# Keys and values in one 512-column product, values in float32, and four late query tiles, in a two-layer encoder

## The chip, the cores and the metric

The kernel runs as one program on one core of a Trainium2 chip. The core has a matrix engine (PE; its weight loads are shown apart as PEld), a vector engine (DVE), a scalar engine (ACT), a general engine (POOL) and a queue that issues the transfers (SP). Each engine works through its own list of instructions in the order in which they were written, and stops at one whose inputs are not there. The metric is the device time of one execution in microseconds (us).

## The reference

The reference is an encoder of two layers on 1024 tokens of width 1024. Layer 0 mixes the tokens with grouped-query attention (16 query heads, 4 key and value heads of 64 columns); layer 1 mixes them with pooled windows. Both layers then attend to 256 memory tokens and end in a gated network with a short convolution. The change touches the attention of layer 0 alone:

```python
qkv = h @ w_qkv
q, k, v = ...            # 16, 4 and 4 heads of 64 columns
q, k = rmsnorm(q, q_gain), rmsnorm(k, k_gain)
q = apply_axial_rope(q, cos, sin) * (HEAD_DIM ** -0.5)
k = apply_axial_rope(k, cos, sin)
p = softmax(q k^T); o = p v; return o @ w_o
```

## The kernel before

**Precision.** A float32 product is made of three products of a "high" and a "low" part: `mm3` (L757 to L759) issues high*high, high*low and low*high. The high part is a copy on ACT (L670, or L688 with a scale), the low part a subtraction on DVE (L673, or L686 with a scale; L950 for the weights).

**Projection.** `attention` first projects the 8 row tiles of 128 tokens. The normalised tokens are not formed; the transposed input is scaled by a column gain and split (`plan_columns`: ACT L688, DVE L686, in chunks of 128, 128, 256 and 512 tokens), and the factor of each row (`first`, from `plan_rows`: a square on ACT L929, two small steps on POOL L931 and L932) is applied to the results. `QKV` lists the products: ("K", t) and ("V", t) are the 256 key and value columns of row tile t, (g, t) a fourth (256 columns, 4 heads) of the queries, ("S", n) a product of queries and keys for the largest scores. Each product is 8 blocks of 128 rows by 3 matrix instructions of 256 columns into a bank pB. Values are split in high and low (L688, L686).

**The head.** A tile of keys or queries then goes through `plan_head`: a square (ACT L1007), a sum over each head (DVE L1011), two small POOL steps (L730, L732), the scaling of the bank by both factors (DVE L1019), the rotation (DVE L1026 twice, L1030) and its sum (POOL L1034). Then PE turns the tile (L1058 for keys, L1089 for queries), and ACT and DVE split it (L670, L673). `LAG` says how many products later the turn is placed. From key tile 2 on the difference of two key tiles (POOL L1052) is turned too. The head takes its tables from `plan_tables` (POOL L899, L906).

**The loop.** The attention itself runs over 16 groups (a half of the rows, a pair of heads), with 8 tiles of keys in each: `plan_scores` (L1221 into pT, the exponential on ACT L1228), `plan_values` (L1263 into pO, in plain float32), `plan_peaks` (L795 into pS, 3 buffers, and the largest score on DVE L801, a group ahead; in the first four steps three of them a step, later two). The values it needs in float32 are formed at its start by `plan_v32`, high plus low, on POOL (L1203). Then come 2000 us of work that the diff does not touch.

**Who sets the order.** `Plan.run` lays out the projection, and then, apart, the loop. It takes PE's work in the written order; an instruction of another engine gets a due time from the PE work that needs it, and one that no PE work of the same plan needs has none and is laid out at the very end. All instructions of the projection therefore stand ahead of all of the loop on each engine. The loop's banks pS, pT and pO lie where the projection's pA and pB lay, and wait for the last reader of what lay there.

## Time and profile before

| what | us |
|---|---|
| median of 3 runs (2408.22 to 2410.0) | 2409.18 |
| the profiled execution | 2408.76 |
| its span on the core | 2407.0 |
| PE busy | 2386.5 |
| DVE busy | 1888.0 |
| ACT busy | 1181.1 |
| POOL busy | 423.4 |
| projection, first product to last | 5.87 to 166.4 |
| loop, first product | 167.51 |

The execution is a little longer than the span of its instructions. A row of the timeline has the start, the time, the engine, the line, the operation, the tiles out<-in and their shape, and in brackets the idle time ahead of it with what ended that. Instructions of PE overlap: the distance between two starts is what one of them costs. The same holds, less strongly, on the other engines.

### The profile page before, as it was taken

Reading aid. Unit: us, or ns where it says so; the run is one execution under the profiler, and the core shown is the slowest. Engines: PE = TensorE matmul, PEld = TensorE weight load, DVE = VectorE, ACT = ScalarE, POOL = GpSimd, SP = SyncE. Lnnn points to the kernel's source line nnn. Section 1 sums busy time; section 2 is a strip of 40 time slices with the busy share of each in tenths; the row PEclk is TensorE's granted clock in tenths of the full one; section 3 lists DMA queues with packets and bytes.
Section 4 is the critical chain, followed back from the end, with each engine's and each line's share of the span. In section 5 each row is a group of like instructions: output and inputs, shape, how many; then the busy total and the mean of one; then the engine's idle time right before and its main releaser. Section 6 shows DMA issues by size and latency. Waiting matters only on the chain.

```text
span 2407.0 us, 33944 instructions
## 1 busy us (share of the span) xinstructions
PE 2386.5 (99%) x12468; PEld 1934.9 (80%) x12468; DVE 1888.0 (78%) x2689; ACT 1181.1 (49%) x1892; POOL 423.4 (18%) x462
## 2 busy tenths in 40 slices
PE   9999999999999999999999999999999999999998
PEld 9984444688998888888888888898888888888887
DVE  6789999549873798888888768987389888888875
ACT  6335556425562555455454426555255555545442
POOL 6757777410010000000000003011000000000001
PEclk9999999999999999999999999999999999999999
DMA  7000001425951234333387533695124332338752
GB/s 255 19 2 11 19 18 42 152 81 194 318 199 44 90 98 128 109 89 109 99 290 248 180 106 123 219 330 201 58 79 120 99 110 88 117 122 274 257 188 101
DMA packets 323010, 324.06 MB, mean 135 GB/s; under 512 B 32564, under 2 KB 253084, under 8 KB 322844
## 3 DMA queue, kind: packets, MB, share of 16 engines
q1 hardware_dynamic: 322844, 321.90, 41.4%
q8 instruction: 98, 1.61, 0.3%
q14 instruction: 68, 0.56, 0.1%
HBM read 234.35 MB, written 82.64 MB: 132 GB/s over the span
## 4 chain that ended last, share of the span: by engine, by line
PE 92%; DVE 3%; issue 3%; DMA 1%; POOL 1%; ACT 1%; SPq 0%; POOLq 0%; DVEq 0%; ACTq 0%
PE pB L757 23%; PE pB L759 23%; PE pB L758 23%; PE pO L1263 4%; PE pT L1221 3%; PE pA L759 3%; PE pA L757 3%; PE pA L758 3%; PE pS L795 2%; PE pB L326 1%; DVE R L673 1%; PE pS L1299 1%; PE pA L2275 1%; DVE nm L801 0%; POOL scr L1275 0%
## 5 line engine op out<-in xcount | busy, mean ns | idle before, releaser
L757 PE MATMUL pB<-R,R 128*128 128x512 f32 (+1 forms) x2764 | 1024.6, 371 | 2.5 <-ACT R L670 0.8
L759 PE MATMUL pB<-R,R 128*128 128x512 f32 (+1 forms) x2760 | 1017.3, 369 | 1.3 <-DVE R L673 1.2
L758 PE MATMUL pB<-R,R 128*128 128x512 f32 (+1 forms) x2764 | 1018.3, 368 | 0.2 <-DVE R L673 0.2
L757 PEld LDWEIGHTS pB<-R,R 128*128 128x128 f32 x2764 | 521.6, 189 | 93.6 <-ACT R L670 2.0
L759 PEld LDWEIGHTS pB<-R,R 128*128 128x128 f32 x2760 | 520.7, 189 | 89.5 <-DVE R L673 3.0
L758 PEld LDWEIGHTS pB<-R,R 128*128 128x128 f32 x2764 | 521.7, 189 | 86.0 <-DVE R L673 1.2
L670 ACT ACTIVATE R<-scr 128x512 fp32r<-128x512 f32 (+3 forms) x372 | 268.6, 750 | 228.4 <-DMA scr<-Gs 61.1
L730 POOL TENSOR_SCALAR ms<-ss 128x1 f32<-128x1 f32 (+1 forms) x92 | 27.1, 294 | 1648.0 <-ACT R L738 1279.0
L673 DVE TENSOR_TENSOR R<-X,R 128x512 fp32r<-128x512 f32 x374 | 252.4, 686 | 67.5 <-ACT R L670 66.9
L673 DVE TENSOR_TENSOR R<-scr,R 128x512 fp32r<-128x512 f32 (+2 forms) x332 | 283.8, 884 | 20.8 <-ACT R L670 20.7
L670 ACT ACTIVATE R<-X 128x512 fp32r<-128x512 f32 x374 | 231.7, 630 | 132.2 <-PE pB L758 64.0
L440 ACT COPY scr<-pB 128x512 f32<-128x512 f32 x156 | 91.3, 585 | 181.6 <-PE pB L759 174.4
L801 DVE TENSOR_REDUCE nm<-pS 128x1 f32<-128x512 f32 x240 | 152.8, 683 | 18.1 <-PE pS L795 16.7
L1966 DVE TENSOR_TENSOR X<-pB,X 128x512 f32<-128x512 f32 (+1 forms) x145 | 99.4, 687 | 84.9 <-PE pB L759 83.9
L1228 ACT ACTIVATE X<-pT 128x1024 f32<-128x1024 f32 x128 | 125.2, 1023 | 76.2 <-PE pT L1221 72.8
L757 PE MATMUL pA<-R,R 128*128 128x512 f32 (+1 forms) x420 | 150.6, 359 | 0.0
L759 PE MATMUL pA<-R,R 128*128 128x512 f32 (+1 forms) x420 | 150.3, 358 | 0.0
L758 PE MATMUL pA<-R,R 128*128 128x512 f32 (+1 forms) x420 | 149.9, 357 | 0.0
L1263 PE MATMUL pO<-X,X 128*64 128x512 f32 x512 | 123.8, 605 | 0.0
L442 DVE TENSOR_TENSOR scr<-pB,scr 128x512 f32<-128x512 f32 x156 | 106.8, 685 | 12.0 <-PE pB L759 11.9
L1221 PE MATMUL pT<-R,R 64*128 64x512 f32 x768 | 104.8, 393 | 1.0 <-ACT X L1228 1.0
L1811 DVE SCALAR_TENSOR_TENSOR scr<-scr,conv 128x1023 f32<-128x1023 f32 x66 | 84.6, 1282 | 20.8 <-ACT scr L1806 19.0
(179 smaller groups left out, 2872.0 us busy)
## 6 DMA issues: line engine op xcount, KB each, us to landing
X<-in_ffn_w_up SPq DMA_DIRECT2D x82, 512.0 KB
Gs<-X SPq DMA_DIRECT2D x105, 256.0 KB
scr<-in_ffn_w_down SPq DMA_DIRECT2D x45, 512.0 KB
scr<-Gs SPq DMA_DIRECT2D x35, 512.0 KB
scr<-in_xattn_w_kv SPq DMA_DIRECT2D x32, 512.0 KB
scr<-Gs SPq DMA_DIRECT2D x42, 384.0 KB
Wt<-scr SPq DMA_DIRECT2D x44, 256.0 KB
Gs<-scr SPq DMA_DIRECT2D x42, 256.0 KB
```

The source lines that it names most:

```text
L440: self.nc.scalar.copy(out, p)
L442: self.nc.vector.tensor_tensor(out=out, in0=p, in1=out, op=OP.add)
L670: self.nc.scalar.activation(hi, src, AF.Copy)
L673: self.nc.vector.tensor_tensor(out=lo, in0=src, in1=hi.bitcast(F32), op=OP.subtract)
L757: mm(out, ah, bh, start=start, stop=False)
L758: mm(out, ah, bl, start=False, stop=False)
L759: mm(out, al, bh, start=False, stop=stop)
L801: nc.vector.tensor_reduce(NM[G][:, 2 * n + x.start:2 * n + x.stop], S, axis=AX.X, op=OP.max, negate=True)
L1221: nc.tensor.matmul(T[G, kt % 2][:, x * 512:(x + 1) * 512], left, right, start=first and (i, j) == (0, 0), stop=shifted or (not first and i ...
L1228: nc.scalar.activation(E[G, kt], T[G, kt % 2], AF.Exp)
L1263: nc.tensor.matmul(O[G][x * HD:(x + 1) * HD], V32[kt // 4][:, kt % 4, m // 4 * 2 + x], E[G, kt][:, x * 512:(x + 1) * 512], start=kt == 0, ...
L1966: nc.vector.tensor_tensor(out=x, in0=banks[b][:, c], in1=x, op=OP.add)
```

## The change

Keys and values of a row tile become one product of 512 columns, so that pB holds both; all 8 of them come first, then the queries. The weights of both come in 8 blocks, each split on ACT and DVE (none of it on POOL any more). The last chunk of tokens, of 512, becomes two of 256. Values are scaled by ACT straight into float32 tiles; their low part and the sum on POOL are gone. The heads of the last four query tiles, (3, 4) to (3, 7), write to one scratch tile, and are turned and split in steps 1 to 4 of the loop, in the place of a bank pS. The three values of `IDLE` that fill PE with transposes at the start change from 8, 15, 4 and 8 to 8, 28 and 4. In the changed file most lines of the attention are lower or higher by some 2 to 18.

```diff
--- before.py
+++ after.py
-QKV = (("K", 0), ("K", 1), ("V", 0), ("V", 1), ("K", 2), ("V", 2), ("K", 3), ("V", 3),
-       ("K", 4), (0, 0), (0, 1), ("K", 5), (0, 2), (0, 3), ("K", 6), (0, 4), (0, 5), ("K", 7), (0, 6), (0, 7),
-       *(it for n in range(24) for it in ([(1 + n // 8, n % 8), ("S", n // 4)] if n % 4 == 1 else [(1 + n // 8, n % 8)])),
-       ("S", 6), ("V", 4), ("S", 7), ("V", 5), ("V", 6), ("V", 7))
-LAG = 4
+QS = [(g, t) for g in range(2) for t in range(NT)] + [(2 + n // 4 % 2, n % 4 + n // 8 * 4) for n in range(2 * NT)]
+QKV = (*(("K", t) for t in range(NT)), *QS[:9], *(it for n, q in enumerate(QS[9:]) for it in ([q, ("S", n // 2)] if n % 2 == 1 and n < 16 else [q])))
+LAG, LATE = 4, 4
 QN = 4
-POOLED = (2, 3)
+POOLED = ()
-IDLE = {("K", 0, 0): 8, **{("K", 0, g): 5 for g in (1, 2, 3)}, ("K", 1, 0): 4, ("K", 2, 0): 8}
-CHUNKS = ((0, P), (P, P), (2 * P, 2 * P), (4 * P, 4 * P))
+IDLE = {("K", 0, 0): 8, **{("K", 0, g): 4 for g in range(1, 8)}, ("K", 1, 0): 4}
+CHUNKS = ((0, P), (P, P), *((n * P, 2 * P) for n in (2, 4, 6)))
...
-        V = [R.get(), None]
+        X = {t: xv.tile([P, D], F32, name=f"XV{t}") for t in (5, 7)}
+        V32 = [X[t].rearrange("p (k h c) -> p k h c", k=4, h=NKV) for t in (5, 7)]
+        late = [(1, NKV - 1, t) for t in range(NT - LATE, NT)]
...
-            sets = [[qk.tile([P, 2048], F32R, name=f"T{i}") for i in range(2)], [R.get(), R.get()], [R.get(), R.get()]]
+            sets = [[qk.tile([P, 2048], F32R, name="T"), R.get()], [R.get(), R.get()], [R.get() for _ in range(4)]]
...
+            def plan_kv(g):
+                raw = ("wraw", "K", g)
+
+                def high(k):
+                    self.high(kv(0)[k // 4][:, k % 4], at[raw][:, k % 2])
+
+                def low(engine, k):
+                    engine.tensor_tensor(out=kv(1)[k // 4][:, k % 4], in0=at[raw][:, k % 2], in1=kv(0)[k // 4][:, k % 4].bitcast(F32),
+                                         op=OP.subtract)
...
+                    if ks[0] == 0:
+                        at[b] = self.psB() if wide else self.psB()[:, :256]
+                        if wide:
+                            at["v", t] = at[b][:, 256:]
+                    for k in ks:
+                        for _ in range(IDLE.get((*it, k), 0) if k == ks[0] else 0):
+                            nc.tensor.transpose(idle[:, :P], self.ident, self.ident)
+                        self.mm3(at[b], *self.blk(hT[t // 4], k, slice(t % 4 * P, (t % 4 + 1) * P)), *weights(k), k == 0, k == NK - 1)
...
+                cut = [(k,) for k in range(NK)] if it == ("K", 0) else [(k, k + 1) for k in range(0, NK, 2)] if it == ("K", 1) else [range(NK)]
...
             def plan_v(t, b):
-                def part(j):
...
-                    self.hi_lo_half(j, v[:, :, :HD], v[:, :, HD:], src(), first[:, t:t + 1])
-                plan.add("copy", 360, partial(part, 0), [b] + own, [("V", t)], uses=[b], room=None if t < 4 else ("V1", 2))
-                plan.add("add", 340, partial(part, 1), [b, ("V", t)] + own, [("V", t)], uses=[b])
+                def scaled():
+                    nc.scalar.activation(V32[t // 4][:, t % 4], at.pop(("v", t)).rearrange("p (h c) -> p h c", h=NKV), AF.Copy, scale=first[:, t:t + 1])
+                plan.add("copy", 360, scaled, [b, ("first", t)], [("V", t)], uses=[b])
...
                 def scaled():
-                    at[qn] = buf("qn", QN) if kind == "Q" else buf("kr", 4)
+                    if it in late:
+                        at["late"] = at["late"] if "late" in at else self.scr()
+                        i = late.index(it)
+                        at[qn] = late[i] = at["late"][:, 256 * i:256 * i + 256]
+                    else:
+                        at[qn] = buf("qn", QN) if kind == "Q" else buf("kr", 4)
...
                 qn, bank = plan_head(it, "Q", t, b), ("qturned", it)
+                if it in late:
+                    return None
...
+            def plan_late(i):
+                b, t = ("late", i), NT - LATE + i
+
+                def turn():
+                    T[b] = self.ps.tile([P, 512], F32, name="pS", bufs=3)
+                    for h in range(2):
+                        nc.tensor.transpose(T[b][:, h * P:(h + 1) * P], late[i][:, h * P:(h + 1) * P], self.ident)
...
+                    self.low(h, l, p) if lo else self.high(h, p)
+                plan.add("turn", 2, turn, [b], [(b, 0)], [("A", b)], ["late"])
...
-            def plan_v32(s):
...
-                    nc.gpsimd.tensor_tensor(out=V32[s], in0=v4[..., :HD], in1=v4[..., HD:], op=OP.add)
...
-                plan.add("product", 9.2, emit, [*es, ("V32", d // 2)], ["O"],
+                plan.add("product", 9.2, emit, es, ["O"],
...
                     if n:
                         plan_values(*steps[n - 1])
+                    if 1 <= n <= LATE:
+                        plan_late(n - 1)
...
-    arrays["attn_w_qkv"] = np.ascontiguousarray(w.transpose(3, 0, 2, 1, 4)).reshape(-1, P, D)
+    kv = w[:, :, :, NKV:].reshape(4, 2, P, 2 * NKV * HD).transpose(0, 2, 1, 3).reshape(-1, P, D)
+    arrays["attn_w_qkv"] = np.concatenate([w[:, :, :, :NKV].transpose(3, 0, 2, 1, 4).reshape(-1, P, D), kv])
```

What it does to the order is seen at three places. The first is DVE at the end of the projection and the start of the loop. Before, from the head of the last query tile on (qn; R9 holds values, R10 turned queries):

```order
L673 TENSOR_TENSOR R10_77<-pB_2347,R10_77 128x2x128
L686 SCALAR_TENSOR_TENSOR R9_76<-pB_2356,first_109,R9_76 128x4x64
L673 TENSOR_TENSOR R10_77<-pB_2396,R10_77 128x2x128
L686 SCALAR_TENSOR_TENSOR R9_76<-pB_2399,first_109,R9_76 128x4x64
L673 TENSOR_TENSOR R10_77<-pB_2444,R10_77 128x2x128
L1193 MEMSET ones_2507 128x64
L686 SCALAR_TENSOR_TENSOR R9_76<-pB_2447,first_109,R9_76 128x4x64
L673 TENSOR_TENSOR R10_77<-pB_2472,R10_77 128x2x128
L801 TENSOR_REDUCE nm_2523<-pS_2511 128x1
L801 TENSOR_REDUCE nm_2523<-pS_2512 128x1
```

After it (L1033, L1040 and L1044 are now the lines of the head, scr_2170 the scratch tile of the late query tiles):

```order
L1020 TENSOR_REDUCE ss4_2246<-sq_2244 128x4
L671 TENSOR_TENSOR R11_78<-pB_2225,R11_78 128x2x128
L1033 SCALAR_TENSOR_TENSOR scr_2170<-pB_2127,first_113,rs_2253 128x256
L1040 TENSOR_TENSOR rb_2256<-scr_2170,tab_111 128x8x16 x2
L1044 TENSOR_TENSOR scr_2170<-scr_2170,tab_111 128x256
L1033 SCALAR_TENSOR_TENSOR scr_2170<-pB_2172,first_113,rs_2263 128x256
L1040 TENSOR_TENSOR rb_2266<-scr_2170,tab_111 128x8x16 x2
L1044 TENSOR_TENSOR scr_2170<-scr_2170,tab_111 128x256
L1033 SCALAR_TENSOR_TENSOR scr_2170<-pB_2200,first_113,rs_2273 128x256
L1040 TENSOR_TENSOR rb_2276<-scr_2170,tab_111 128x8x16 x2
L1044 TENSOR_TENSOR scr_2170<-scr_2170,tab_111 128x256
L802 TENSOR_REDUCE nm_2314<-pS_2303 128x1
```

Three heads of late query tiles stand between the projection's last turned tile and the loop's first largest score, each behind the POOL steps (rs) of its own; before, value parts stood there.

The second is PE at the same place, with what each instruction waits for. Before:

```order
L759 MATMUL pB_2447<-T0_105,R15_82 128x256
L1089 MATMUL pB_2472<-ident_87,qn_2390 128x128 [waits DVE_49,PE_49,Pool_49]
L1089 MATMUL pB_2472<-ident_87,qn_2390 128x128
L795 MATMUL pS_2511<-R0_67,R16_83 128x512 [waits DVE_49]
L795 MATMUL pS_2512<-R0_67,R16_83 128x512
L1221 MATMUL pT_2516<-R16_83,R0_67 128x512 [waits DVE_49]
```

After:

```order
L757 MATMUL pB_2200<-R4_71,R17_84 128x256
L1105 MATMUL pB_2225<-ident_87,qn_2119 128x128 [waits DVE_49,Activation_49,Pool_49]
L1105 MATMUL pB_2225<-ident_87,qn_2119 128x128
L796 MATMUL pS_2303<-R0_67,R18_85 128x512 [waits DVE_49,Activation_49]
L796 MATMUL pS_2304<-R0_67,R18_85 128x512 [waits PE_49]
L1239 MATMUL pT_2307<-R18_85,R0_67 128x512 x4
```

The first product of the loop now waits for ACT too. Counted in the program, the instruction of DVE that it waits for is the scaling of the last late tile (L1033 out of pB_2200, the third L1033 in the DVE rows above), since pS_2303 lies in a bank of that tile; before, it was the low part of the last value tile (L686 out of pB_2447).

The third is DVE early in the projection, at the heads of key tiles 0 and 1 (kr) and the next chunk of tokens (R with gcol). Before:

```order
L1011 TENSOR_REDUCE ss4_431<-sq_380 128x4
L1030 TENSOR_TENSOR kr_390<-kr_390,scr_300 128x256
L686 SCALAR_TENSOR_TENSOR R3_70<-pB_287,first_109,R3_70 128x4x64
L686 SCALAR_TENSOR_TENSOR R3_70<-pB_334,first_109,R3_70 128x4x64
L1019 SCALAR_TENSOR_TENSOR kr_443<-pB_245,first_109,rs_436 128x256
L1026 TENSOR_TENSOR rb_449<-kr_443,scr_300 128x8x16 x2
L1030 TENSOR_TENSOR kr_443<-kr_443,scr_300 128x256
L1011 TENSOR_REDUCE ss4_484<-sq_445 128x4
L686 SCALAR_TENSOR_TENSOR R13_80<-scr_425,gcol_108,R12_79 128x512 x2
L686 SCALAR_TENSOR_TENSOR R13_80<-scr_438,gcol_108,R12_79 128x512
```

After:

```order
L1033 SCALAR_TENSOR_TENSOR kr_397<-pB_160,first_113,rs_383 128x256
L1033 SCALAR_TENSOR_TENSOR kr_429<-pB_268,first_113,rs_395 128x256
L684 SCALAR_TENSOR_TENSOR R15_82<-scr_374,gcol_112,R14_81 128x256
L1040 TENSOR_TENSOR rb_438<-kr_397,scr_370 128x8x16 x2
L1040 TENSOR_TENSOR rb_442<-kr_429,scr_370 128x8x16 x2
L1044 TENSOR_TENSOR kr_397<-kr_397,scr_370 128x256
L1044 TENSOR_TENSOR kr_429<-kr_429,scr_370 128x256
L1020 TENSOR_REDUCE ss4_452<-sq_433 128x4
L684 SCALAR_TENSOR_TENSOR R15_82<-scr_374,gcol_112,R14_81 128x256 x3
L684 SCALAR_TENSOR_TENSOR R17_84<-scr_385,gcol_112,R16_83 128x256 x4
L1033 SCALAR_TENSOR_TENSOR kr_490<-pB_342,first_113,rs_470 128x256
```

The chunk for row tiles 4 and 5 (R15, R17), eight instructions, now stands behind the heads of both key tiles, and ahead of it all key and value products of the first four row tiles; before, two value tiles stood between the heads.

169 lines of the change are left out of this document (76 added, 93 removed).

## Prediction, made before the run

> **What bounds the kernel now.** The page first, for the bound of the whole: its span, and the chain that ended last.
>
> ```profile
> span 2407.0 us, 33944 instructions
> PE 92%; DVE 3%; issue 3%; DMA 1%; POOL 1%; ACT 1%; SPq 0%; POOLq 0%; DVEq 0%; ACTq 0%
> ```
>
> PE carries 92% of the chain. So a change counts by the PE work that it takes away and by the time in which PE waits. The profiled execution took 2408.76 us, 0.4 below the median of 2409.18; the sum is made against it. 0.2% (4.8 us) is about what a measurement of this kernel can tell from no change.
>
> Next the timeline of PE at the two ends of the projection, since the diff changes nothing behind the loop's second group.
>
> ```profile
> 5.87 0.36 PE L757 MATMUL pB<-T,R 128*128 128x256 f32 x1
> ...
> 6.98 0.71 PE L972 MATMUL pB<-ident 128*128 128x128 f32 x5
> 7.45 0.36 PE L757 MATMUL pB<-T,R 128*128 128x256 f32 x1
> ...
> 12.65 0.60 PE L972 MATMUL pB<-ident 128*128 128x128 f32 x4
> ...
> 22.99 0.28 PE L758 MATMUL pB<-T,R 128*128 128x256 f32 x1
> ...
> 25.20 0.28 PE L759 MATMUL pB<-T,R 128*128 128x256 f32 x1
> 27.43 0.44 PE L1058 MATMUL pB<-ident,kr 128*128 128x128 f32 x2 [1.95 <-POOL kr L1034]
> ...
> 163.23 0.38 PE L1089 MATMUL pB<-ident,qn 128*128 128x128 f32 x2
> 166.26 0.38 PE L1089 MATMUL pB<-ident,qn 128*128 128x128 f32 x2
> 167.51 0.50 PE L795 MATMUL pS<-R,R 64*128 64x512 f32 x2 [0.87 <-DVE R L686]
> ```
>
> The first key tile takes from 5.87 to 12.65, mostly waits and filling transposes; at 25.2 PE waits 2.1 us from start to start for POOL; after that it runs without a gap until the loop's first product at 167.51, which waits for a value part.
>
> ```profile
> 28.48:31.68 3.20, 3.20 (x16) 3.20 (x16) 2.93 (x5) 2.68 (x6) 3.03 (x4) 0.50 0.19 26
> 160.00:170.00 10.00, 9.13 (x78) 8.57 (x77) 7.16 (x21) 3.15 (x7) 4.95 (x5) 1.00 0.07 2
> 170.00:180.00 10.00, 9.79 (x54) 4.64 (x53) 9.97 (x17) 5.25 (x6) 1.29 (x1) 1.00 0.00 0
> ```
>
> These are stretches: length, then busy time of PE, PEld, DVE, ACT and POOL, and the granted clock. Soon after the wait at 25 the clock was 0.50 for 3.2 us, and 16 products took that long instead of 16 x 0.116 = 1.9; the wait so cost another 1.3 us (one clock window, below). At the loop's start DVE is busy for 9.97 of 10 us: the first group hangs on it as much as on PE.
>
> **The change, part by part.** The pace of products comes from two rows above and two of a later stage:
>
> ```profile
> 600.16 0.39 PE L759 MATMUL pB<-R,R 128*128 128x512 f32 x1
> 600.39 0.39 PE L757 MATMUL pB<-R,R 128*128 128x512 f32 x1
> ```
>
> From 22.99 to 25.20 there are 19 steps: 0.116 us for 256 columns. For 512 it is 0.227. Keys and values were 16 tiles x 24 x 0.116 = 44.5 us and become 8 x 24 x 0.227 = 43.6: a gain of 0.9. The wide product as such is worth little, since the narrow one was already nearly twice as fast.
>
> The four query turns that leave the projection: a tile with its turn takes 166.26 - 163.23 = 3.03 us, its products 24 x 0.116 = 2.78, the turn 0.25; a gain of 1.0 there, given back in the loop.
>
> PE's lost time among the keys. Before: the first tile 6.8 less 2.8 is 4.0; two more filling groups 12 x 0.094 = 1.1 (five take 7.45 - 6.98 = 0.47); the wait 2.1; the slow clock 1.3; together 8.5. After it, the queues have to be followed, with these rows:
>
> ```profile
> 3.54 4.99 DMA scr<-in_attn_w_qkv
> ...
> 11.58 7.41 DMA scr<-in_xt
> ```
>
> ```profile
> 9.09 3.60 ACT L688 ACTIVATE R<-scr,gcol 128x128 fp32r<-128x128 f32 x12
> ...
> 17.77 1.03 ACT L929 ACTIVATE pA<-scr 128x1024 f32<-128x1024 f32 x1 [0.39 <-DMA scr<-in_x]
> ...
> 19.02 3.31 ACT L688 ACTIVATE R<-scr,gcol 128x256 fp32r<-128x256 f32 x8
> ```
>
> ```profile
> 16.85 1.29 POOL L899 TENSOR_TENSOR scr<-tab,gk 128x512 f32<-128x512 f32 x1
> 18.10 0.88 POOL L906 TENSOR_TENSOR scr<-tab,gk 128x128 f32<-128x128 f32 x2
> ...
> 19.06 0.19 POOL L931 TENSOR_SCALAR ms<-ss 128x1 f32<-128x1 f32 x1
> 19.33 0.56 POOL L932 TENSOR_TENSOR first<-ms,mh 128x1 f32<-128x1 f32 x1
> ...
> 25.39 0.20 POOL L730 TENSOR_SCALAR ms<-ss 128x4 f32<-128x4 f32 x1
> 25.67 1.02 POOL L732 TENSOR_TENSOR rs<-ms,mh 128x4 f32<-128x4 f32 x1
> ...
> 28.32 0.74 POOL L1034 TENSOR_TENSOR kr<-kr,rb 128x256 f32<-128x256 f32 x1 [0.68 <-DVE kr L1030]
> 29.14 0.52 POOL L730 TENSOR_SCALAR ms<-ss 128x4 f32<-128x4 f32 x1
> ```
>
> ```profile
> 19.56 3.69 DVE L686 SCALAR_TENSOR_TENSOR R<-scr,gcol,R 128x256 fp32r<-128x256 f32 x8 [1.72 <-ACT R L688]
> ...
> 26.72 0.48 DVE L1019 SCALAR_TENSOR_TENSOR kr<-pB,first,rs 128x256 f32<-128x256 f32 x1 [1.03 <-POOL rs L732]
> 27.24 0.53 DVE L1026 TENSOR_TENSOR rb<-kr,scr 128x128 f32<-128x128 f32 x2
> 27.81 0.43 DVE L1030 TENSOR_TENSOR kr<-kr,scr 128x256 f32<-128x256 f32 x1
> ...
> 31.70 1.05 DVE L1026 TENSOR_TENSOR rb<-kr,scr 128x128 f32<-128x128 f32 x2
> ```
>
> The transfers (the chain of waits) had brought 1.5 MB of tiles by 8.53 and 5.5 MB by 18.99, 0.38 MB a us. The first product now needs 2.5 MB instead of 1.5, so its last weights land near 11.1; the second token chunk follows near 12.5. The first tile then goes at its own pace: 24 x 0.227 = 5.4, 28 filling transposes x 0.094 = 2.6, and some 0.9 of waits at the first two blocks: it ends at 14.8 (loss 3.5). Four more fillers (0.4) and three wide tiles follow to 31.5, the turn of two key tiles to 32.0.
>
> The fifth tile needs its token chunk, whose low parts stand on DVE behind the heads of the first two. ACT comes from 12.5 through 8 short splits (0.30 each), a row square (1.2), 8 splits (0.41) and another square to 20.6. POOL then works through the second row's factor (0.9), the first part of the key table (1.29 and 0.88), the first key head (1.3), another row's factor (0.9), the second head (1.3) and the rest of the table (0.9): 28.1. DVE then needs 2 x 0.5 and 2 x 0.35 for the rotations, 0.35 for a sum, and 7 low parts at 0.46: 33.4, or 33.9 if one rotation runs as slowly as that at 31.70 next to POOL. PE waits 1.4 to 1.9 us; I take 1.8. A slow clock after it is as likely as not: bounds 0 (the short waits of the first tile brought none) and 1.3; I take 0.7. The later chunk comes some 3 us early by the same counting. Lost after: 3.5 + 0.4 + 1.8 + 0.7 = 6.4, a gain of 2.1. Bounds: 0.4 more gain without the slow rotation and 0.7 without a slow clock; on the other side 2 less, if each of the POOL steps is as slow as the slowest of its kind.
>
> Value low parts on DVE, POOL's sum of values, and the weight parts that go from POOL to DVE cost nothing on the path: early on DVE waits for transfers and for POOL by the counting above, and at the loop's start DVE, not POOL, is the full engine (9.97 against 1.29 of 10 us). If that cover is gone, the weight parts cost 2 x 0.7 on DVE. The queries, 32 tiles of some 3 us, keep their pace: the next row shows PE without a gap over most of them, with DVE at 79%.
>
> ```profile
> 80.00:160.00 80.00, 80.00 (x655) 76.71 (x654) 62.80 (x156) 22.13 (x53) 55.94 (x78) 1.00 0.01 2
> ```
>
>
> So the last product of the projection ends 0.9 + 1.0 + 2.1 = 4.0 us earlier, at 162.4 instead of 166.4. Call that end T.
>
> **The start of the loop.** Here stands what the change adds.
>
> ```profile
> 166.97 0.48 DVE L686 SCALAR_TENSOR_TENSOR R<-pB,first,R 128x256 fp32r<-128x256 f32 x1 [2.14 <-ACT R L688]
> 167.37 0.41 DVE L673 TENSOR_TENSOR R<-pB,R 128x256 fp32r<-128x256 f32 x1
> 168.04 7.32 DVE L801 TENSOR_REDUCE nm<-pS 128x1 f32<-128x512 f32 x12 [0.26 <-PE pS L795]
> ```
>
> Before, DVE was through 1.3 us after T, and PE began the loop at T + 1.1. Now three late heads stand on DVE behind the last turned tile, and their steps go back and forth: DVE scales, rotates, POOL sums, and only then POOL's two steps for the next head, since they stand behind that sum. One such round, from the rows at 26.72 to 29.14: 1.60 from the scaling to POOL's sum, 0.82 to the next small step, 0.28 and 1.05 (25.39 to 26.72) to the next scaling: 3.75 us. The first scaling starts at T + 1.3, the third at T + 8.8. PE's first product of the loop waits for that third scaling: T + 9.3 instead of T + 1.1, a loss of 8.2 us. Bounds: 7.0 with the rounds at their bare busy times, 9.5 with POOL's longer small step. Queued behind that product is all of the loop; the ACT exponentials and DVE's largest scores wait with it. Nothing gives the time back: behind it PE and DVE have 9.79 and 9.97 us of work in 10.
>
> After some 9 us without work the clock will be low again: 1.3 us by the stretch at 28.48; bounds 0 (DVE sets the pace in part of that time) and 2.6 (two stretches). [...]
>
> The four late turns: 4 x 0.25 = 1.0 on PE, with DVE's four low parts at 0.33 beside them (167.37 and what follows in its kind), where DVE is full: 1.0 to 2.3, I take 1.2.
>
> Sum: -4.0 + 8.2 + 1.3 + 1.2 = +6.7, so 2408.8 + 6.7 = 2415.5 us. The likeliest case by itself: 2411 to 2419.
>
> **The rivals.**
>
> The late heads hide: the bank of the loop's first product, or the heads' place on POOL, lets PE begin as before. For it: DVE had 21% to spare among the queries, and was idle for 2.14 us ahead of 166.97. Against it: the order of the instructions, which no engine can change. Then 8.2 and 1.3 fall away: 2406.0, faster than before; by more than 0.2% if also the keys run without the wait (2403.5). It decides from the point where the first product of the loop starts within 3 us of T. Chance 0.20 (0.12 faster by over 0.2%, 0.08 within).
>
> The keys run at PE's pace and the clock stays up: no wait at 32, no slow clock there or in the loop, and the late turns lie beside DVE's work. For it: several of the POOL durations were stretched by DVE beside them. That takes 1.8 + 0.7 + 1.3 + 1.0 off: 2410.7, within 0.2%. Chance 0.23.
>
> POOL becomes the bound of the key tiles: the work of 8 heads, 8 row factors and two tables, which before lay over 50 us, now lies over some 45; POOL had 3.03 of 3.20 us busy at 28. Each later turn then waits 1 us, for five turns, less what is already in the sum: 2419. The clock staying low over two stretches gives 2416.8 by itself. Chance 0.15.
>
> [...]
>
> **How the numbers follow.** The forecast has 0.42: 0.33 of it above 0.2%, 0.09 within, as its low end of 2411 lies inside. Slower: 0.33 + 0.15 = 0.48. Within: 0.09 + 0.23 + 0.08 = 0.40. Faster: 0.12. The range reaches down to 2405 (the hidden heads in part) and up to 2421 (POOL as the bound, with two slow stretches), and leaves out about 0.15.
>
> **What would show it.** The projection's last product ends near 162; the page shows PE's largest wait, about 8 us, on the first product of the loop, released by DVE's scaling of the late heads (line 1033 of the new file) or by the POOL steps before it; a low clock in the stretch behind it; a PE wait of 1 to 2 us near 32 on DVE's low parts; the steady groups of the loop unchanged. I am wrong if the first product of the loop follows T within 3 us, or if the projection ends before 158 or after 166.

## The result, and the profile after

| | before | after |
|---|---|---|
| median of six runs each, us | 2410.19 (2408.22 to 2410.68) | 2418.92 (2417.30 to 2421.08) |
| ratio | 1 | 1.0038, 95% interval 1.0025 to 1.0051 |
| the profiled execution, us | 2408.76 | 2417.89 |
| its span, us | 2407.0 | 2416.1 |

The changed kernel is slower by 0.38%, 8.7 us. The page after (its span and the chain that ended last), and from the groups by line the loop's largest scores, whose columns are count, busy time, mean ns, and PE's idle time ahead of them with what ended it:

```profile
span 2416.1 us, 33574 instructions
PE 91%; issue 3%; DVE 3%; POOL 2%; DMA 1%; ACT 1%; SPq 0%; POOLq 0%; DVEq 0%; ACTq 0%
...
L796 PE MATMUL pS<-R,R 64*128 64x512 f32 x240 | 58.9, 452 | 9.7 <-DVE scr L1033 9.0 <-DVE nm L802 0.6
```

On the chain POOL has 2% instead of 1%. PE waits 9.0 us in one place for DVE's scaling of a late head. The timeline of PE shows where: the last turn of the projection, the loop's first product, and the first product with values.

```profile
162.73 0.38 PE L1105 MATMUL pB<-ident,qn 128*128 128x128 f32 x2
172.09 0.80 PE L796 MATMUL pS<-R,R 64*128 64x512 f32 x2 [8.97 <-DVE scr L1033]
...
179.94 1.94 PE L1281 MATMUL pO<-X,XV 128*64 128x512 f32 x8
```

Before, the first two stood at 166.26 and 167.51, and the first product with values at 174.05. So the projection ends 3.5 us earlier, and the loop starts 4.6 us later. What lies between, on DVE and on POOL:

```profile
164.11 0.47 DVE L1033 SCALAR_TENSOR_TENSOR scr<-pB,first,rs 128x256 f32<-128x256 f32 x1
...
167.78 0.48 DVE L1033 SCALAR_TENSOR_TENSOR scr<-pB,first,rs 128x256 f32<-128x256 f32 x1 [2.21 <-POOL rs L730]
...
171.46 0.48 DVE L1033 SCALAR_TENSOR_TENSOR scr<-pB,first,rs 128x256 f32<-128x256 f32 x1 [2.21 <-POOL rs L730]
```

```profile
165.65 0.72 POOL L1048 TENSOR_TENSOR scr<-scr,rb 128x256 f32<-128x256 f32 x1 [5.61 <-DVE scr L1044]
166.46 0.19 POOL L728 TENSOR_SCALAR ms<-ss 128x4 f32<-128x4 f32 x1
166.73 1.01 POOL L730 TENSOR_TENSOR rs<-ms,mh 128x4 f32<-128x4 f32 x1
```

Three scalings, 3.67 us apart. In each round POOL forms the sum of one head before its two small steps for the next, and DVE stands idle for 2.21 us. The granted clock over the same stretch (length, then busy time of PE, PEld, DVE, ACT and POOL, then the clock):

```profile
161.63:165.04 3.41, 1.49 (x13) 1.25 (x11) 1.56 (x5) 0.75 (x2) 0.00 (x0) 1.00 0.00 0
165.04:175.28 10.24, 3.19 (x16) 2.76 (x18) 4.83 (x14) 0.65 (x1) 4.57 (x7) 0.50 0.00 0
175.28:178.69 3.41, 3.15 (x23) 1.82 (x21) 3.35 (x6) 1.74 (x3) 0.00 (x0) 1.00 0.00 0
```

The first 3.2 us of the loop, from 172.09 to 175.28, run at a clock of 0.50. Among the key tiles, PE's timeline reads (a filler is a transpose of the identity that only keeps PE busy; the eight ahead of the first tile, the four ahead of its last block, the four with which the second tile begins, then the waits at three key turns):

```profile
5.15 1.04 PE L989 MATMUL pB<-ident 128*128 128x128 f32 x8
...
14.79 0.60 PE L989 MATMUL pB<-ident 128*128 128x128 f32 x4
15.94 0.60 PE L989 MATMUL pB<-ident 128*128 128x128 f32 x4
33.73 0.44 PE L1072 MATMUL pB<-ident,kr 128*128 128x128 f32 x2 [0.61 <-POOL kr L1048]
46.88 0.44 PE L1072 MATMUL pB<-ident,dk 128*128 128x128 f32 x2 [1.05 <-POOL dk L1066]
59.45 0.44 PE L1072 MATMUL pB<-ident,dk 128*128 128x128 f32 x2 [0.53 <-POOL dk L1066]
```

The first tile ends at 15.9, the waits behind it sum to 2.2 us, and the granted clock stays at 1.00 behind them, up to 165.0.

### The profile page after: what moved, and what is told of

It is laid out like the page before. It is cut to its first block, busy times and chain, and to the rows that moved or that the text cites. A ratio compares the mean times of both kernels' runs of the same rounds, so it can differ in the third digit from the quotient of the medians.

```text
span 2416.1 us, 33574 instructions
## 1 busy us (share of the span) xinstructions
PE 2388.5 (99%) x12281; PEld 1925.2 (80%) x12281; DVE 1885.5 (78%) x2691; ACT 1180.3 (49%) x1900; POOL 415.3 (17%) x458
## 4 chain that ended last, share of the span: by engine, by line
PE 91%; issue 3%; DVE 3%; POOL 2%; DMA 1%; ACT 1%; SPq 0%; POOLq 0%; DVEq 0%; ACTq 0%
PE pB L755 23%; PE pB L756 23%; PE pB L757 23%; PE pO L1281 4%; PE pT L1239 3%; PE pA L757 3%; PE pA L755 3%; PE pA L756 3%; PE pS L796 2%; PE pB L324 1%; DVE R L671 1%; PE pS L1317 1%; PE pA L2293 0%; POOL rs L730 0%; POOL scr L1293 0%
## 5 line engine op out<-in xcount | busy, mean ns | idle before, releaser
L671 DVE TENSOR_TENSOR R<-scr,R 128x512 fp32r<-128x512 f32 (+2 forms) x336 | 289.5, 889 | 25.1 <-ACT R L668 24.3
L671 DVE TENSOR_TENSOR R<-X,R 128x512 fp32r<-128x512 f32 x258 | 175.5, 688 | 48.3 <-ACT R L668 47.9
L668 ACT ACTIVATE R<-X 128x512 fp32r<-128x512 f32 x258 | 160.9, 630 | 97.8 <-PE pB L756 48.3
L1281 PE MATMUL pO<-X,XV 128*64 128x512 f32 x512 | 123.8, 605 | 0.0
L1984 DVE TENSOR_TENSOR X<-pB,X 128x512 f32<-128x512 f32 (+1 forms) x109 | 74.7, 686 | 62.1 <-PE pB L757 61.3
```

What stands on the lines that cost most here:

```text
L668: self.nc.scalar.activation(hi, src, AF.Copy)
L671: self.nc.vector.tensor_tensor(out=lo, in0=src, in1=hi.bitcast(F32), op=OP.subtract)
L1281: nc.tensor.matmul(O[G][x * HD:(x + 1) * HD], V32[kt // 4][:, kt % 4, m // 4 * 2 + x], E[G, kt][:, x * 512:(x + 1) * 512], start=kt == 0, ...
```

## The experiments

Every kernel was run beside the kernel before on the same chip. The first table shows medians and, for the change itself, the result above; the second how late each profile is against the profile before at four places: the first product with values (a step of eight instructions into pO), the fifth (one group on), the ninth (two groups on), and the end of the execution. The intervals reach 2 to 3 us to either side, so a difference of 1 us between two medians tells nothing by itself; there the argument rests on the places in the profiles. The starts before were 174.05, 193.33 and 210.30, the end 2408.76.

| kernel | median, us | before beside it | difference | ratio, 95% interval |
|---|---|---|---|---|
| the change | 2418.92 | 2410.19 | 8.7 | 1.0025 to 1.0051 |
| e1_due | 2413.33 | 2409.32 | 4.0 | 1.0010 to 1.0028 |
| e2_no_late | 2414.89 | 2409.32 | 5.6 | 1.0016 to 1.0034 |
| e3_warm | 2417.88 | 2409.32 | 8.6 | 1.0025 to 1.0050 |
| e4_narrow | 2419.20 | 2409.32 | 9.9 | 1.0029 to 1.0056 |
| e7_warm80 | 2416.43 | 2408.95 | 7.5 | 1.0023 to 1.0047 |
| e8_drain | 2413.40 | 2408.95 | 4.5 | 1.0011 to 1.0029 |
| e6_due_idle1 | 2415.70 | 2408.95 | 6.8 | 1.0017 to 1.0038 |
| e5_due_differ | 2414.58 | 2408.95 | 5.6 | 1.0012 to 1.0030 |
| e9_urgent | 2414.72 | 2409.61 | 5.1 | 1.0012 to 1.0030 |
| e10_later | 2413.90 | 2409.61 | 4.3 | 1.0011 to 1.0030 |
| e11_fill | 2414.83 | 2409.94 | 4.9 | 1.0014 to 1.0032 |
| e12_fill_later | 2414.19 | 2409.94 | 4.3 | 1.0007 to 1.0025 |

| profile | first | fifth | ninth | end |
|---|---|---|---|---|
| the change | 5.89 | 7.54 | 7.57 | 9.13 |
| e1_due | 1.81 | 3.45 | 3.46 | 4.25 |
| e2_no_late | 4.06 | 4.07 | 4.07 | 5.90 |
| e3_warm | 5.61 | 7.26 | 7.27 | 9.12 |
| e4_narrow | 6.66 | 8.29 | 8.28 | 9.89 |
| e7_warm80 | 4.66 | 6.31 | 6.34 | 6.11 |
| e8_drain | 0.03 | 1.66 | 1.67 | 4.61 |
| e6_due_idle1 | 3.56 | 5.21 | 5.23 | 7.04 |
| e5_due_differ | 3.58 | 5.21 | 5.21 | 7.26 |
| e9_urgent | 2.15 | 4.29 | 4.29 | 5.25 |
| e10_later | 2.35 | 2.36 | 4.09 | 4.06 |
| e11_fill | 0.20 | 1.82 | 1.83 | 4.12 |
| e12_fill_later | 0.42 | 0.43 | 2.16 | 3.69 |

**Is the order of the late heads the wait?** The heads' seven steps get due times when their tile is late:

```diff
+                due = lambda x: x if deferred else None
-                plan.add("scale", 2.9, rstd, [ss], [ss])
+                plan.add("scale", 2.9, rstd, [ss], [ss], late=due(2.5))
...
```

> The steps of the heads of the four late query tiles get due times, so that all of them stand in the order of DVE and POOL ahead of, or between, the first steps of the loop by urgency, and POOL's small steps of one head no longer stand behind POOL's sum of the head before. Nothing is computed differently. Theory (the wait for the third late head's scaling is the loss): the loop's first product starts about 3 us after the projection's last turn instead of 9.2 us, so 6.3 us are gained if the clock drops as before, 7.6 if it now stays up: 2411 to 2413 us where the changed kernel has 2418.9. Rival (the key phase, or the work of the late turns, is the loss, and DVE is so full at the loop's start that a wait taken away at one place comes back at the next): the first product is earlier, but the first pO product of the loop stays within 2 us of its place, and the time within 2 us of 2418.9.

PE's last turn, and the first two products of the loop:

```profile
162.28 0.38 PE L1106 MATMUL pB<-ident,qn 128*128 128x128 f32 x2
165.78 0.76 PE L796 MATMUL pS<-R,R 64*128 64x512 f32 x1 [3.12 <-DVE scr L1034]
167.67 0.79 PE L796 MATMUL pS<-R,R 64*128 64x512 f32 x1 [1.13 <-DVE R L671]
```

The wait fell from 9.0 to 3.1 us with nothing computed differently, but a second one of 1.1 us came behind it, for low parts that the due times had pushed back. By the medians 4.7 us were gained of the 6.3 expected (8.7 less 4.0). The theory holds for 5.9 of the 9.0 us of wait: a wait of 3.1 us for the same scaling is left. The new wait is 1.1 of the missing 1.6 us, and the clock fell here too (0.50 from 165.18 to 172.00).

**What do late tiles cost in all?**

```diff
-LAG, LATE = 4, 4
+LAG, LATE = 4, 0
```

(The tile held for late heads in the loop is left out with them.)

> No query tile is turned late: all of them are turned in the projection, as in the kernel before; the wide key and value product, the values as float32 and everything else of the change stay. Theory (late heads and late turns cost about 9 us together with the slow clock, the rest of the change gains about 4): PE waits at the projection's last turns for the heads of the last tiles, some 4 to 5 us in all, since the heads' steps then are waited for where they stand, and the loop starts right behind them; about 4 us less than the changed kernel, 2414 to 2416. Rival (the late turns are a gain, as the place where they are put hides the heads' round): the time is over 2420. If the heads' round is no cost at all, the time is 2409 or less.

```profile
166.03 0.44 PE L1105 MATMUL pB<-ident,qn 128*128 128x128 f32 x2 [2.31 <-POOL qn L1048]
166.71 0.44 PE L1105 MATMUL pB<-ident,qn 128*128 128x128 f32 x2 [0.24 <-POOL qn L1048]
168.39 0.69 PE L1105 MATMUL pB<-ident,qn 128*128 128x128 f32 x2 [1.24 <-POOL qn L1048]
169.51 0.80 PE L796 MATMUL pS<-R,R 64*128 64x512 f32 x2 [0.43 <-DVE R L671]
```

As expected: 4.2 us of waits at the projection's end, and 3.1 us less than the change, where 4 were expected. The clock fell here too, to 0.50 between 168 and 174. It is still 5.6 us slower than before, which hid the last heads behind value tiles. And it gives a term by itself: without late turns the first group of the loop takes what it took before (4.06 at its start, 4.07 at its end); with them in the first group it grows by 1.62 to 1.65 in every kernel but one (e9_urgent, where the slow clock reached into it: its first eight products with values took 2.37 us, 1.87 in e10_later).

**What does the slow clock cost?** 64, then 80 transposes of the identity behind the projection's last product:

```diff
                 main()
+                idle = self.psB()
+                for _ in range(64):
+                    nc.tensor.transpose(idle[:, :P], self.ident, self.ident)
```

> 64 transposes of the identity into an unused PSUM bank are added on PE behind the projection's last product; they take some 6 us of the 9 us in which PE only waits. Nothing else is changed: the wait for the late head's scaling stays where it is. Theory (the cold clock behind the wait costs 1.3 us, bounds 0 and 2.6): the first product of the loop still starts some 9.2 us after the projection's last turn, the granted clock behind it stays at 1.00, and the time is 1 to 2.5 us below 2418.9. Rival (DVE sets the pace there, the slow clock costs nothing): the clock stays up and the time is within 0.7 us of 2418.9. Third case: transposes do not keep the clock up, and the row of the clock reads as before.

With 64 of them (PE's timeline, then two stretches):

```profile
162.87 7.15 PE L1194 MATMUL pB<-ident 128*128 128x128 f32 x64
172.03 0.50 PE L796 MATMUL pS<-R,R 64*128 64x512 f32 x2 [2.01 <-DVE scr L1033]
```

```profile
169.81:173.22 3.41, 1.40 (x12) 1.17 (x11) 1.75 (x6) 0.00 (x0) 1.66 (x4) 1.00 0.00 0
173.22:176.64 3.42, 3.24 (x16) 1.82 (x13) 2.58 (x5) 1.59 (x2) 0.46 (x1) 0.50 0.02 5
```

None of the three expectations: with the transposes the clock was 1.00 up to the loop and into it, to 173.22, and then it fell all the same, to 0.50 for 3.4 us, with 2.0 of the 3.41 us ahead still idle. The gain was nothing.

> As the run with 64 transposes of the identity behind the projection's last product, with 80 of them: at 0.112 us each they take 8.9 us and so cover the whole wait of PE, while the loop's first product stays where it was. In the run with 64, PE was idle for 2.0 us behind them and the clock fell to 0.50 all the same, for 3.4 us from 1.2 us after the loop's start. Theory (a stretch of 3.4 us in which PE is idle for some 2 us lowers the clock in the next one): with under 0.5 us of idle time the clock stays at 1.00 from 160 to 185, the first pO product starts 1.3 us earlier against the projection's end than in the changed kernel, and the time is 1.3 us lower, 2417 to 2418. Rival (transposes do not count, and the clock falls again): row and time as in the changed kernel, 2418.9. Second rival (DVE sets the pace behind the wait): the clock stays up and the first pO product is where it was.

With 80:

```profile
162.84 8.90 PE L1194 MATMUL pB<-ident 128*128 128x128 f32 x80
172.00 0.50 PE L796 MATMUL pS<-R,R 64*128 64x512 f32 x2 [0.26 <-DVE scr L1033]
```

```profile
172.00:182.00 10.00, 9.79 (x58) 5.29 (x58) 9.63 (x18) 4.49 (x5) 0.73 (x1) 1.00 0.01 2
```

The clock stays at 1.00. The first product with values comes 1.23 us earlier than in the change, 0.11 of it from the earlier end of the projection; the medians differ by 1.2 (8.7 and 7.5), which alone would not tell. So the slow clock behind the wait cost 1.1 to 1.2 us.

**Is the wide product worth anything?** Its two halves as two products in the same place:

```diff
-                        self.mm3(at[b], *self.blk(hT[t // 4], k, slice(t % 4 * P, (t % 4 + 1) * P)), *weights(k), k == 0, k == NK - 1)
+                        for c in (slice(0, 256), slice(256, 512)) if wide else (slice(0, 256),):
+                            self.mm3(at[b][:, c], *self.blk(hT[t // 4], k, slice(t % 4 * P, (t % 4 + 1) * P)),
+                                     *(x[:, c] for x in weights(k)), k == 0, k == NK - 1, wide)
```

In this kernel the two halves of a bank are begun apart, and the sums in them are not those of the reference; number, size and place of the instructions are as told.

> The product of keys and values is issued as two products of 256 columns each in the same place and order of the work, into the two halves of the same bank: 48 instead of 24 for each row tile. Theory (the pace of 256 columns is 0.116 us and of 512 columns 0.227, so the wide form by itself is worth little): 8 x 24 x (2 x 0.116 - 0.227) = 1.0 us more, of which part is hidden by the waits of the first tile: 2419 to 2420. Rival (the wide product is what made the projection shorter): the projection ends 3 to 4 us later and the time is 2422 or more.

```profile
PE pB L1074 <- POOL dk L1068: 0.4, 1, 0.4
PE pB L1074 <- POOL kr L1050: 0.3, 1, 0.3
```

9.9 us against 8.7 for the change; the projection's last turn stands at 163.32, 0.6 us later, and PE's waits for POOL at the key turns fell from 2.2 to 0.7 us. So the narrow form takes 2.1 us more of PE's time at this place (0.6 and 1.5), twice the 1.0 worked out, and 1.5 of it falls into time in which PE had waited for POOL. The forecast took its two paces, 0.116 and 0.227, from rows of other places. Here, between two key turns, 24 wide products run from 39.91 to 45.22, 0.231 from start to start, and 48 narrow ones from 40.86 to 46.57, 0.1215. What lasts is 0.6 us at the projection's end and 0.8 in the profile.

**Can the key tiles go faster?** Both with the due times of e1_due: one filler instead of four for each block of the first tile, and the difference of keys on DVE.

```diff
-IDLE = {("K", 0, 0): 8, **{("K", 0, g): 4 for g in range(1, 8)}, ("K", 1, 0): 4}
+IDLE = {("K", 0, 0): 8, **{("K", 0, g): 1 for g in range(1, 8)}, ("K", 1, 0): 4}
```

> Due times as before, and one filling transpose instead of four ahead of each block of the first key tile. Theory (the first tile runs at its own pace, 0.68 us of products and 0.11 us for each filler, so that the fillers are on the path): 7 x 3 x 0.11 = 2.3 us less for the first tile, so a projection that ends up to 2.3 us earlier than with due times alone, 2411 us, if the clock stays at 1.00; with one stretch of slow clock, 2412.5. Rival (transfers and the splitting of weights set the pace of the first tile, or POOL that of the key tiles behind it): the first tile ends earlier by less than 1 us, or PE gives it back in waits ahead of the fourth to sixth key tile, and the time is within 0.7 us of 2413.3.

```profile
9.48 0.50 PE L755 MATMUL pB<-R,R 128*128 128x512 f32 x1 [1.28 <-ACT R L686]
...
34.62 0.44 PE L1073 MATMUL pB<-ident,kr 128*128 128x128 f32 x2 [1.61 <-POOL kr L1049]
```

```profile
35.20:38.60 3.40, 3.40 (x10) 2.66 (x9) 2.81 (x9) 2.56 (x7) 3.15 (x5) 0.51 0.88 306
```

The rival's mechanism held, and the loss went beyond its 0.7 us: the first tile ends 0.4 us earlier than in e1_due (15.04 against 15.44) instead of 2.3, since the fillers had mostly filled time in which PE would have waited for ACT's splits; a later wait for POOL grew from 0.7 to 1.6 us, and a stretch of slow clock followed it. 2.7 us slower than with due times alone (6.75 and 4.01 by the medians).

```diff
-                    nc.gpsimd.tensor_tensor(out=at[dk], in0=at[kr[t]], in1=at[kr[t - 2]], op=OP.subtract)
+                    nc.vector.tensor_tensor(out=at[dk], in0=at[kr[t]], in1=at[kr[t - 2]], op=OP.subtract)
```

> Due times as before, and the difference of two key tiles is formed on DVE instead of POOL. Theory (POOL, busy for 31 of 40 us between 20 and 60, paces the turns of the key tiles in the changed kernel, by 2.2 us of waits in all): PE's waits on POOL's key steps fall from 2.2 to under 1 us, the projection ends 1 to 2 us earlier than with due times alone, and the time is 2411.5 to 2412.5. Rival (DVE, with 0.35 us more for each of six tiles, is as late with the differences): the waits move to DVE and the time is within 0.7 us of 2413.3.

```profile
34.82 0.44 PE L1073 MATMUL pB<-ident,kr 128*128 128x128 f32 x2 [1.62 <-POOL kr L1049]
41.96 0.44 PE L1073 MATMUL pB<-ident,kr 128*128 128x128 f32 x2 [1.22 <-POOL kr L1049]
42.90 0.44 PE L1073 MATMUL pB<-ident,dk 128*128 128x128 f32 x2 [0.51 <-DVE dk L1067]
```

Neither expectation: the planner laid the steps out anew, and PE's waits grew to 3.4 us. POOL was busy for 27.1 of 40 us instead of 31.6 while PE's waits grew, so its load alone does not set them; that it is the place of a head's steps in its row is likely, but was not tried by itself. 1.6 us slower than with due times alone.

**Is it the bank, or the head?** ACT copies the four late products out of PSUM, and the heads start from that copy; low parts of the last turned tiles get due times too.

```diff
+                    nc.scalar.activation(at[qn], at.pop(b), AF.Copy, scale=first[:, t:t + 1])
...
+                    if deferred:
+                        nc.vector.tensor_tensor(out=q3(), in0=q3(), in1=at.pop(ss)[:, :, None].to_broadcast([P, 4, HD]), op=OP.mult)
+                        return
```

> The products of the four late query tiles are copied out of PSUM by ACT into the tile that holds them anyway, right behind the product, and their heads are worked out from there; the heads have the due times of the earlier run, and the low parts of the last three turned tiles get due times too. Theory (what the loop's first product waits for is the PSUM bank in which the third late head's product stands, not the head itself): the first product starts within 1.5 us of the projection's last turn, PE's idle time there falls from 9.0 us (4.2 us with due times alone) to under 2 us, and the time is 2 to 4 us below the 2413.3 with due times alone: 2409.5 to 2411.5. Rival (DVE, full at the loop's start, is what is waited for in the end, as the heads' steps still stand on it): the first product is early, but the first pO product is no more than 0.5 us earlier than with due times alone, and the time is 2413.

PE at the end of the projection, and DVE's last nine of the first twelve largest scores with what follows:

```profile
163.99 0.44 PE L1112 MATMUL pB<-ident,qn 128*128 128x128 f32 x2 [1.41 <-POOL qn L1053]
166.00 0.79 PE L796 MATMUL pS<-R,R 64*128 64x512 f32 x2 [1.57 <-DVE R L671]
```

```profile
170.00 5.39 DVE L802 TENSOR_REDUCE nm<-pS 128x1 f32<-128x512 f32 x9
175.32 1.21 DVE L1298 TENSOR_TENSOR scr<-X,X 128x1024 f32<-128x1024 f32 x1
```

The wait for the late head is gone: PE waits 3.0 us in two other places. But the first product with values stands where it stood before, 174.08, though the projection's products end 3.7 us earlier (163.99 less the wait of 1.41 is 162.58; before, 166.26). DVE is through its twelfth largest score at 170.00 + 5.39 = 175.39; before it was at 168.04 + 7.32 = 175.36. From 166.52 to that end DVE's row has no idle time; ahead of it stand two waits of 0.57 us for POOL's factors. So DVE, with the late heads among its scores, sets the start of the loop. Neither expectation fits whole: the wait for the bank went as the theory said, but PE's waits fell to 3.0 us and not under 2; and the first product with values came 1.8 us earlier than with due times alone, where the rival allowed 0.5, but the time is the rival's 2413. The rest of this kernel's 4.6 us in the profile: 1.63 for the late turns, 2.6 at the loop's end (below) and 0.4 behind it.

**Do the last waits go, too?** From e8_drain, the tiles (2, 4) to (2, 7) get the late tiles' due times:

```diff
-                due = lambda x: x if deferred else None
+                due = lambda x: x if deferred or (kind, *it[:2]) == ("Q", 1, NKV - 2) else None
```

> As the run with products copied out of PSUM, and the heads of the last four tiles that are turned in the projection get due times like the late ones, so that these no longer pass them on DVE and POOL: in the run before, PE waited 1.4 us at the projection's last turn for POOL's sum of the last turned tile, and 1.6 us at the loop's first product for DVE's low parts. Theory (what the late turns lose at the loop's start is waits in the order of DVE and POOL and the slow clock behind them, nothing of the work itself): both waits fall below 0.5 us, the clock stays at 1.00 from 160 to 180, the first pO product starts 2.5 to 4 us earlier than in the run before, and the time is 2409 to 2411. Rival (DVE and POOL have more to do there than PE, so the waits come back at the first largest scores): the first pO product is less than 1.5 us earlier, and the time is 2412 or more.

```profile
168.92 0.49 PE L796 MATMUL pS<-R,R 64*128 64x512 f32 x1 [3.14 <-DVE nm L802]
...
170.86 2.00 PE L796 MATMUL pS<-R,R 64*128 64x512 f32 x3 [0.43 <-DVE nm L802]
```

The rival held: PE starts the loop without a wait and then waits 3.1 us for the first largest score, which stands behind the heads on DVE; the clock fell as well: six score products took 1.45 us to the next start behind the waits (172.07 to 173.52), 0.79 ahead of them (164.38 to 165.17).

**The turns in the loop's second group,** from e9_urgent.

```diff
-                    if 1 <= n <= LATE:
-                        plan_late(n - 1)
+                    if 5 <= n < 5 + LATE:
+                        plan_late(n - 5)
```

> As the run above, with the four late turns behind steps 5 to 8 of the loop instead of steps 1 to 4. In every run with late turns so far, the first four steps of values grew by 1.62 to 1.65 us together against the kernel before, and by 0.06 without late turns; the turns themselves are 4 x 0.25 = 1.0 us on PE in the projection. Theory (the rest, 0.65 us, is DVE's work of the first group, where DVE is the full engine): the first four steps take what they took before, the next four 1.0 us more, and the time is 0.3 to 0.8 us below the run above. Rival (PE alone carries them, 0.4 us for each turn anywhere): the time is that of the run above within 0.3 us.

```profile
197.55 0.44 PE L1221 MATMUL pS<-ident,scr 128*128 128x128 f32 x2
197.92 0.50 PE L796 MATMUL pS<-R,R 64*128 64x512 f32 x2
```

The first group takes 19.29 us (176.40 to 195.69), as before; the second grows by 1.73. So the theory fell by the places: the 0.65 us that were to be DVE's did not go away. It is PE's own time, 0.4 us a turn in either group: PE has no wait in the second one, and a turn takes 0.37 us to the next start. By the medians this kernel is 0.8 us below e9_urgent, as the theory said and outside the rival's 0.3, but that difference is within the spread, and e9_urgent's first group held slow clock besides (2.37 us for its first eight products with values, 1.87 here).

**A last attempt at a faster version**, from e8_drain: the factor applied by the operation that took 0.48 us in the change, 10 fillers ahead of the loop, and then the turns in the second group.

```diff
-                        nc.vector.tensor_tensor(out=q3(), in0=q3(), in1=at.pop(ss)[:, :, None].to_broadcast([P, 4, HD]), op=OP.mult)
+                        nc.vector.scalar_tensor_tensor(q3(), q3(), 1.0, at.pop(ss)[:, :, None].to_broadcast([P, 4, HD]), op0=OP.mult, op1=OP.mult)
```

> As the run with products copied out of PSUM (2413.4; its first pO product stood where it stands in the kernel before, but PE's waits there brought a stretch of slow clock), with two edits: the heads' factors are applied by the operation with a scalar and a tensor (0.48 us in the earlier runs) instead of the one with two tensors (0.95 us in that run), and 10 filling transposes stand on PE ahead of the loop's first product, where PE waited 1.6 us. Theory (DVE's order sets the start of the loop, the clock takes the rest): DVE's twelfth largest score, at 175.3 in both the kernel before and that run, ends some 1 to 1.4 us earlier, the clock stays at 1.00, and the time is 2410.5 to 2412. Rival (the heads' latency over ACT, DVE and POOL sets it, not DVE's busy time): the first pO product moves by less than 0.5 us and the time is 2413.

POOL and DVE at one late head of this kernel, and then of e1_due, where the source is PSUM:

```profile
163.35 0.72 POOL L1053 TENSOR_TENSOR qn<-qn,rb 128x256 f32<-128x256 f32 x1
...
163.41 0.94 DVE L1034 SCALAR_TENSOR_TENSOR scr<-scr,rs 128x256 f32<-128x256 f32 x1 [0.57 <-POOL rs L730]
```

```profile
165.09 0.72 POOL L1049 TENSOR_TENSOR scr<-scr,rb 128x256 f32<-128x256 f32 x1
...
165.16 0.48 DVE L1034 SCALAR_TENSOR_TENSOR scr<-pB,first,rs 128x256 f32<-128x256 f32 x1 [1.18 <-POOL rs L730]
```

The first product with values did not move (174.25), as the rival said, but its cause was not put to the test, since DVE's work did not shrink: the operation takes 0.94 us whichever of the two it is. It starts 0.06 us behind a sum on POOL and ends 0.28 us behind the end of that sum. From PSUM, beside the same sum, it takes 0.48. The clock stayed at 1.00: in e8_drain the slow clock lay beside DVE's work (six score products took 1.29 us to the next start at 166.59, 0.80 at 171.27), and with or without it the first product with values stands within 0.2 us of the same place.

> As the run above, with the four late turns behind steps 5 to 8 of the loop instead of steps 1 to 4. In the earlier pair of runs that differ in this alone, the growth over the loop's first two groups fell from 1.65 us to what the next row will show here, but their profiles differed in the key tiles too. Theory (0.65 of 1.65 us is DVE's work in the first group): the first four steps of values take what they take in the kernel before, the next four some 1.0 us more, and the time is 0.3 to 0.8 us below the run above. Rival (PE alone carries the turns): within 0.3 us of the run above.

The first group as before (0.42 and 0.43), the second longer by 1.73: the same as in e10_later, now in a pair of profiles that start the loop within 0.2 us of each other. At the ninth product this kernel is 0.3 us behind e11_fill; its median is 0.6 below, again within the spread. Its interval, 1.0007 to 1.0025, is still slower than before. None of these versions beats the kernel before.

**The loop's end.** Between the ninth product with values and 500 us the profiles lose unequally, in code that no edit touches, around one wait of PE for ACT; e2_no_late and e12_fill_later:

```profile
442.47 0.96 PE L1237 MATMUL pT<-R,R 64*128 64x512 f32 x6 [1.74 <-ACT X L1244]
```

```profile
441.56 0.96 PE L1250 MATMUL pT<-R,R 64*128 64x512 f32 x6 [1.71 <-ACT X L1257]
```

The wait was 0.99 us before and 1.56 in the change. Measured up to the same group of transposes near 500 us (498.03 before), 1.7 to 2.6 us are lost where a stretch of slow clock follows the wait (the 16 products with values behind it took 5.18 us in e8_drain and 4.90 in e9_urgent, against 3.49 in e10_later without it; e9_urgent 1.7, e5_due_differ 2.0, e8_drain, e2_no_late and e6_due_idle1 2.6); where none does, from 0.5 gained to 1.0 lost (e4_narrow -0.5, e10_later 0, e12_fill_later 0.8, the change 0.9, e11_fill 1.0). Another 0.7 us is lost by the change behind that, in small steps up to 1840 us; why these places differ from profile to profile was not tried.

## Why the prediction was right

The direction, and the steps that carry it, held. By its own terms:

- **The wide product, -0.9:** the right sign, mis-sized. e4_narrow shows 2.1 us of PE's time among the key tiles, of which 1.5 is waited away in this kernel.
- **Key tiles, -2.1, and the projection's end at 162.4:** it ended at 162.9 (the last turn at 162.73), a gain of 3.5 instead of 4.0. The step that the first tile ends at 14.8 was too early by 1.1 us: a filler costs (15.94 - 14.79 - 3 x 0.227) / 4 = 0.117 us beside the wide products, not 0.094, which makes 0.6 us for 28; and the first product came 0.4 later, at 6.24 instead of 5.87. The wait of 1.8 us near 32 for DVE's low parts did not come; 2.2 us of waits for POOL's key steps at three turns took its place, which is the third rival's mechanism at a smaller size. The slow clock of 0.7 did not come. That the sum of the projection is off by only 0.5 us is in part luck: a wide product worth more than told, a slower first tile, a wait at another place and a slow clock that stayed away nearly cancel.
- **The start of the loop, +8.2:** 8.1. The rounds take 3.67 us, 3.75 were worked out, and the first product stands 9.2 us behind the projection's end, as forecast. e1_due shows that the order of POOL's and DVE's steps is the cause of 5.9 of the 9.0 us of wait.
- **The slow clock, +1.3:** 1.1 to 1.2 by e7_warm80.
- **The four late turns, +1.2:** mis-sized. They cost 1.65, by e2_no_late against the others, within the bounds of 1.0 to 2.3. The price of a turn, 0.25 us, was read in the projection; in the loop a turn costs 0.4. It is PE's time and not DVE's fullness, since in the second group, where PE waits for nothing, the cost is the same.

With these sizes the profile after should be -3.5 + 8.1 + 1.2 + 1.65 = 7.45 us later at the end of the first group, and it is 7.54 later. The other 1.6 us up to the end of its execution are outside the prediction's terms: 0.9 up to 500 us and 0.7 behind. The median lies 3.4 us above the 2415.5 forecast: 0.8 for the terms (7.5 against 6.7), 1.6 for what lies outside them, and 1.0 since the profiled execution was that much below its median. The first rival, that the late heads hide, failed as told: "the order of the instructions, which no engine can change". The prediction named DVE as full there, but its rival held that without the wait the loop would begin early and 9.5 us would fall away. The runs show less: with the wait for the late head gone, in e8_drain and e11_fill, PE begins the loop at 166.00 and 166.15 instead of 167.51, and the first product with values stands where it stood before, with DVE's row full up to its twelfth largest score. In e9_urgent it came 2.2 us later still, with slow clock. How much of this is DVE's busy time and how much the heads' way over POOL (two waits of 0.57 us) was not separated.

## What to carry to other kernels

Work that is moved off one engine's path takes its helpers with it: the four turns weighed 1 us on PE, but their heads' steps on DVE and POOL came to stand at the one place where DVE was full (9.97 of 10 us before), and what had hidden their latency, the value tiles, had been merged away. Before work is deferred across the border of two stages, look at which engine is full on the other side and at what each queue holds between. And price an operation in the stage that it moves to: the same turn cost 0.25 us in one and 0.4 in the other.

## What the runs showed of the hardware

- The slow clock, 0.50, came in stretches of about 3.41 us or multiples: 3.41 before (28.34 to 31.75, the stretch that the prediction counts as one clock window), 3.42 in e3_warm, 6.82 in e1_due (165.18 to 172.00), 10.24 in the change. PE had not been idle for the whole 3.4 us ahead of it: for 1.95 of 3.40 us before (24.94 to 28.34), 1.9 of 3.41 in the change, 2.0 of 3.41 in e3_warm.
- At the loop's end waits of 1.7 us went either way: a slow stretch followed waits of 1.66 and 1.74 us in two profiles (1.74 in e2_no_late), and none followed waits of 1.71 to 1.80 in five (1.71 in e12_fill_later, 1.73 in e10_later). One followed waits of 1.86 to 1.90 us in all three profiles that had them (1.86 in e8_drain, 1.90 in e9_urgent), and none waits of 1.56 us and less in four (1.56 in the change, 0.99 before).
- With 80 transposes of the identity on PE for 8.9 us ahead of the loop (e7_warm80) the clock was 1.00 over the loop's first 10 us (172.00 to 182.00); in the change, where PE waited 9.0 us there, it was 0.50 for the first 3.2 of them.
- The scaling of a head with two inputs in the SBUF took 0.94 us on DVE beside POOL's sum (e11_fill), 0.28 of it behind the sum's end; with one input in PSUM it took 0.48 beside the same sum (e1_due). Why the first took longer was not shown. With the products copied out of PSUM early, the scaling of a late head took 0.46 us more.
